# Scratch for rotary queries, laid out by part instead of by head

## The chip, the cores and the metric

The kernel runs on one core of a Trainium2 chip. A core has a matrix engine (PE, TensorE) with a loader for its stationary operand (PEld), a vector engine (DVE), an activation engine (ACT), a general engine (POOL) and a small engine that here only starts transfers (SP). SP, ACT and POOL start DMA transfers; the transfers themselves run on the core's 16 DMA engines. Every engine works through its own list of instructions in order, so an instruction that waits holds up all that stand behind it on the same engine.

The metric is the time of the whole program on the device, in microseconds (us), as the median of several executions.

## The reference

The program is one inference step of a two-layer decoder trunk: 1024 new prompt tokens and 8 sample tokens share the weights. Layer 0 mixes tokens with an mLSTM, layer 1 with multi-head latent attention; each layer ends with a SwiGLU network. The change touches the attention layer alone, and there the queries of the prompt:

```python
c_q, c_kv, k_r = jnp.split(x @ w_in, [Q_LORA, Q_LORA + KV_LORA], axis=-1)
q = (rmsnorm(c_q, g_q) @ w_uq).reshape(B, S, MLA_HEADS, QK_NOPE + QK_ROPE)
q_nope = q[..., :QK_NOPE]                       # 8 heads x 128
q_rope = rope(q[..., QK_NOPE:], pos)            # 8 heads x 64: two halves of 32, turned by the position
s = einsum('bqhc,bkc->bhqk', q_lat, c_kv) + einsum('bqhr,bkr->bhqk', q_rope, k_r)   # q_lat is q_nope @ w_uk
```

Behind it come a causal softmax in blocks of 128 queries, the product with the values, and the output projection. All is float32. The kernel gets the precision on PE by splitting a number into a high part that PE takes as it is and the low rest, so that most products are three matmuls (high x high, low x high, high x low).

## The kernel before, in words

Activations lie transposed, features on the 128 partitions and tokens along the row. The prompt's tokens are worked in three chunks of 344 columns, of which the last holds 336 prompt tokens and the 8 sample tokens.

**The stage of the queries** (`queries`, from L1307) runs through the table `ORDER = "R0 P1 P2 P3 R4 P5 P6 P7 A0"`. `P` makes the plain part of one head (`plain`): three chunks of 9 matmuls. `R0` and `R4` make the rotary part of four heads at once, 4 heads x 32 rows on the partitions, once for each half `e` (`rotary`), besides the plain part of their own head. Each chunk's result goes through `keep` (L1322): ACT writes the high part and DVE the low part of a buffer `qx`, of which there are 12, and then `put_n` (L1331) or `put_r` (L1336) stores it to scratch in DRAM: plain parts to `qn_d`, rotary parts to `qr_d`. A buffer is free for the next chunk when its store has landed. The stores of an entry are issued with the next entry. SP issues the plain stores of heads 0 to 3 and the rotary stores of `R4`; POOL issues the rotary stores of `R0` and the plain stores of heads 4 to 7. Each rotary chunk takes two stores for each half, `i` = 0 for the high and 1 for the low part.

`qr_d` is `[8, P, S]` before: head, then 128 rows, then position. The rows of a head are four parts of 32: high first half, high second half, low first half, low second half (row `64 * i + 32 * e + r`). A store therefore writes 4 heads x 32 rows.

**The attention** (`attention`, from L1446) works in 32 blocks, 8 heads x 4 groups `G` of 256 queries. `load_q` (L1465) fetches a block's queries, one transfer for the plain part (`q`, L1470) and one for the rotary part (`qrr`, 128 rows x 256 columns, L1471), each into one of two buffers. For head 0 ACT issues them, for the others SP, and they are asked for one block ahead. In `prompt` (L1519) the scores take `q` at L1544 to L1546 and `qrr` at L1547 and L1549, with a mask at L1551; DVE takes the maximum (L1552), ACT the exponential (L1561) and the scaling (L1566), PE transposes (L1582) and multiplies with the values (L1602). Between the blocks stand the next head's keys and values (`head_ops`: ACT writes `kt`, `vt` and `spl` at L125 and L126, POOL the low parts at L127) and units for the sample tokens (`sample_units`: gathers from the paged cache on POOL, transposes on DVE, matmuls at L1706 and L1731). `sample_query` (L1406) stands between queries and attention: 16 small matmuls from `qnS` (L1419) and 16 copies of ACT to `qbd` (L1426).

The order of the instructions on each engine isn't written out by hand: a scheduler settles it when the program is built, from priorities and its own costs. A change of a transfer's shape or number can therefore move other instructions.

Of the kernel before, what the change touches and what calls it, by code (L numbers as in the profile page):

```python
# [9 lines left out]
F32 = mybir.dt.float32  # L10
# [8 lines left out]
P = 128  # L19
D = 1024  # L20
KT = D // P
S = 1024
# [66 lines left out]
class Kern:  # L89
# [1217 lines left out]
    def queries(self, qs, cq):  # L1307
        nc = self.nc
        V = nc.vector
        cqh, cql, rc, rn, wT = cq  # L1310
        self.qn_d = self.t(self.dp, [8, 2, P, S], "qn_d")
        self.qr_d = self.t(self.dp, [8, P, S], "qr_d")
        wuq = self.mla_w_uq[0]
        self.qnS = self.t(qs, [P, 8, NS], "qnS")
        self.qrS = self.t(qs, [64, 8, NS], "qrS")
# [17 lines left out]
        def put_r(h0, e):  # L1333
            def f(x, w):
                for i in range(2):
                    (nc.sync if h0 else nc.gpsimd).dma_start(self.qr_d[h0:h0 + 4, 64 * i + 32 * e:64 * i + 32 * e + 32, w], x[:, i])  # L1336
            return f


# [50 lines left out]
        for op in ORDER.split():  # L1390
            h = int(op[1:] or 0)
# [54 lines left out]
    def attention(self, ckh, ckl, kk, kl, cqp, cq):  # L1446
        nc = self.nc
# [17 lines left out]
        def load_q(h, G):  # L1465
            g = slice(G * 256, G * 256 + 256)
            q = self.t(pe, [P, 2, 256], "q", F32R, bufs=2)
            x = self.t(pe, [P, 256], "qrr", F32R, bufs=2)
            e = nc.scalar if h == 0 else nc.sync
            e.dma_start(q.bitcast(F32), self.qn_d[h, :, :, g].rearrange("i p s -> p i s"))  # L1470
            e.dma_start(x.bitcast(F32), self.qr_d[h, :, g])  # L1471
            return q, x

        def head_ops(h):
# [44 lines left out]
        def prompt(h, G, kt, vt):  # L1519
            hv = slice((h % 2) * P, (h % 2) * P + P)  # L1520
            nk = 2 * G + 2

            slot = h * 4 + G if h % 2 == 0 or h == 7 else h * 4 + 3 - G
            q, qx = ahead.pop(slot, None) or load_q(h, G)
            n = slot + 1
            if 0 < slot < 31:
                ahead[n] = load_q(n // 4, n % 4 if n // 4 % 2 == 0 or n >= 28 else 3 - n % 4)
# [393 lines left out]
```

## Time and profile before

| what | us |
|---|---|
| executions, fastest / median / slowest of 3 | 2754.57 / 2765.08 / 2766.46 |
| span of the profiled execution (first to last instruction; its whole time isn't listed apart) | 2743.8 |
| PE busy in the span | 2578.0 (94%) |
| DVE / ACT / POOL busy | 1497.8 / 1178.1 / 877.8 |
| stage of the queries, 1335.0 to 1410.7 | 75.7, PE busy 59.65 |
| 32 blocks of attention, 1410.7 to 1888.0 | 477.3, PE busy 418.04 |

The span is shorter than an execution by what lies before the first and behind the last instruction: 10.8 us against the fastest run, 21.3 us against the median. In views that list instructions, a row has start and duration in us, engine, line, operation, output and inputs; square brackets hold how long the engine sat idle before it, and what ended that. An engine's name with a q (SPq, ACTq) is its sequencer, which issues transfers. Windows give each engine's busy time in a stretch, with the clock that PE was granted (1.00 is full), the busy share of the 16 DMA engines and what they moved.

### The profile page before, as it was taken

To read this page: it belongs to the slowest core of one execution; us is meant where nothing else is said; L and a number is where in the kernel's file an instruction comes from. 1 tells how busy PE (TensorE), PEld (TensorE's weight loads), DVE (VectorE), ACT (ScalarE), POOL (GpSimd) and SP (SyncE) were. 2 spreads that over 40 slices of the span, in tenths; PEclk is the share of its full clock that TensorE was granted. 3 is DMA by queue.
4 is the path that set the end of the run, shared out by engine and by line. 5 is a ranking of instruction groups with operands and counts; after the bars stand their busy time and mean duration, and the time that the engine had idled before them with its cause. 6 is when DMAs were issued, how large, how long until landed. Compare 5 with 4: busy or idle time off the path is not lost.

```text
span 2743.8 us, 51995 instructions
## 1 busy us (share of the span) xinstructions
PE 2578.0 (94%) x20719; PEld 2439.0 (89%) x20719; DVE 1497.8 (55%) x3217; ACT 1178.1 (43%) x2651; POOL 877.8 (32%) x846
## 2 busy tenths in 40 slices
PE   8999988989999999999888889898988999999998
PEld 8998877989999999999776767777988999999998
DVE  4345668863343443366548876686574434444455
ACT  4212334444444444453345455555344444444442
POOL 1000002233333333332325544452223333333343
PEclk9999989999999999999889999898999999999999
DMA  5133455426666556543657767664434655555553
GB/s 186 39 77 92 124 145 128 147 60 128 122 122 120 117 115 123 105 158 102 201 177 293 247 242 242 212 220 150 145 92 99 124 116 123 117 115 116 118 139 103
DMA packets 344937, 384.27 MB, mean 140 GB/s; under 512 B 24362, under 2 KB 296111, under 8 KB 336375
## 3 DMA queue, kind: packets, MB, share of 16 engines
q0 software_dynamic: 42496, 183.35, 28.0%
q1 hardware_dynamic: 277990, 181.25, 22.6%
q10 hardware_dynamic: 24208, 16.36, 2.4%
q8 instruction: 162, 2.65, 0.4%
q14 instruction: 81, 0.66, 0.1%
HBM read 255.17 MB, written 125.70 MB: 139 GB/s over the span
## 4 chain that ended last, share of the span: by engine, by line
PE 66%; DVE 12%; DMA 10%; issue 5%; ACT 4%; POOL 3%; SPq 0%; ACTq 0%; POOLq 0%; DVEq 0%
PE sc L133 10%; PE sc L131 10%; PE sc L132 10%; PE mm L131 5%; PE mm L133 5%; PE mm L132 5%; PE ss L131 5%; PE ss L132 5%; PE ss L133 5%; DVE tt L1699 2%; DMA Gb<-G_d 2%; PE ss L1731 2%; DVE wl L115 1%; DMA nat<-in_cache_latent_dram,idx 1%; DMA qr_d<-qx 1%
## 5 line engine op out<-in xcount | busy, mean ns | idle before, releaser
L131 PE MATMUL ss<-ah,dh 128*128 128x344 f32 x864 | 276.8, 320 | 7.1 <-ACT st L1075 6.7
L1075 ACT COPY st<-ss 128x344 f32<-128x344 f32 x432 | 190.2, 442 | 212.9 <-PE ss L133 173.1
L132 PE MATMUL ss<-al,dh 128*128 128x344 f32 x864 | 276.6, 320 | 1.9 <-POOL al L115 1.9
L133 PE MATMUL ss<-ah,dl 128*128 128x344 f32 x864 | 275.9, 319 | 0.0
L114 ACT ACTIVATE wh<-wr 128x512 fp32r<-128x512 f32 (+2 forms) x152 | 126.1, 830 | 228.2 <-PE mm L132 130.0
L1077 POOL DMA_DIRECT2D x_d<-st x144 | 124.5, 864 | 238.6 <-ACT st L1075 229.1
L131 PEld LDWEIGHTS ss<-ah,dh 128*128 128x128 f32 x864 | 162.4, 188 | 8.3 <-ACT st L1075 7.3
L115 POOL TENSOR_TENSOR al<-u,ah 128x512 fp32r<-128x512 f32 (+1 forms) x84 | 118.2, 1408 | 147.3 <-ACT ah L114 147.2
L132 PEld LDWEIGHTS ss<-al,dh 128*128 128x128 f32 x864 | 162.8, 188 | 2.4 <-POOL al L115 2.4
L115 DVE TENSOR_TENSOR wl<-S,wl 128x512 fp32r<-128x512 f32 x89 | 78.4, 881 | 157.1 <-ACT wl L114 129.4
L133 PEld LDWEIGHTS ss<-ah,dl 128*128 128x128 f32 x864 | 162.3, 188 | 0.0
L1699 DVE STREAM_TRANSPOSE tt<-nat 128x1024 f32<-128x1024 f32 x128 | 153.1, 1220 | 14.5 <-DMA nat<-in_cache_latent_dram,idx 9.3
L1041 DVE TENSOR_TENSOR u<-u,sc 128x260 f32<-128x260 f32 (+1 forms) x168 | 70.8, 421 | 115.2 <-PE sc L133 113.9
L115 DVE TENSOR_TENSOR wh<-S,wh 128x512 fp32r<-128x512 f32 x91 | 68.6, 754 | 119.0 <-ACT wh L114 90.2
L115 DVE TENSOR_TENSOR wl<-wr,wh 128x1024 fp32r<-128x1024 f32 (+2 forms) x83 | 100.2, 1208 | 43.1 <-ACT wh L114 35.2
L1007 POOL TENSOR_TENSOR S<-S,wr 128x512 f32<-128x512 f32 x45 | 62.9, 1398 | 175.0 <-DVE wl L115 88.5
L1000 POOL TENSOR_TENSOR S<-wr 128x512 f32<-128x512 f32 x45 | 61.6, 1369 | 166.0 <-DMA wr<-in_ffn_w_gate_up_dram 163.3
L131 PE MATMUL mm<-zh,wh 128*128 128x344 f32 x320 | 104.6, 327 | 7.6 <-DVE ot L459 7.5
L115 DVE TENSOR_TENSOR dl<-dr,dh 128x256 fp32r<-128x256 f32 x144 | 68.3, 474 | 72.7 <-ACT dh L114 72.7
L132 PE MATMUL mm<-zl,wh 128*128 128x344 f32 x320 | 103.6, 324 | 0.0
L133 PE MATMUL mm<-zh,wl 128*128 128x344 f32 x320 | 103.3, 323 | 0.0
L1009 POOL TENSOR_TENSOR S<-S,wr 128x512 f32<-128x512 f32 x45 | 58.1, 1291 | 132.9 <-DVE wh L115 86.5
(920 smaller groups left out, 9279.0 us busy)
## 6 DMA issues: line engine op xcount, KB each, us to landing
x_d<-st POOLq DMA_DIRECT2D x144, 516.0 KB, 5.6
wr<-in_ffn_w_gate_up_dram SPq DMA_DIRECT2D x98, 512.0 KB
dr<-in_ffn_w_down_dram SPq DMA_DIRECT2D x144, 128.0 KB
wr<-in_mlstm_w_in_dram SPq DMA_DIRECT2D x24, 512.0 KB
wr<-in_mlstm_w_out_dram SPq DMA_DIRECT2D x16, 512.0 KB
wr<-in_mla_w_o_dram SPq DMA_DIRECT2D x15, 512.0 KB
q<-qn_d SPq DMA_DIRECT2D x28, 256.0 KB
x_d<-x SPq DMA_DIRECT2D x16, 260.0 KB
```

The lines of the kernel that those rows point to most:

```text
L114: ins = nc.scalar.activation(hi, src, AF.Copy)
L115: self.low = e.tensor_tensor(lo, src, hi.bitcast(F32), op=ALU.subtract)
L131: mm(ps, wh, xh, start=start, stop=False, **kw)
L132: mm(ps, wh, xl, start=False, stop=False, **kw)
L133: self.last = mm(ps, wl, xh, start=False, stop=stop, **kw)
L1000: G(s, a21, a22, op=ALU.add)
L1007: G(s, s, a11, op=ALU.subtract)
L1009: G(s, s, a12, op=ALU.subtract)
L1041: V.tensor_tensor(u[:, 1], u[:, 1], ps, op=ALU.add)
L1075: nc.scalar.copy(st[:, cs], ps)
L1077: nc.gpsimd.dma_start(self.x_d[:, d], st, accum_op=ALU.add)
L1699: V.transpose(out=tt, in_=src.rearrange("p s (c i) -> p c s i", i=32))
```

## The change

The scratch for the rotary queries becomes `[4, 8 * 32, S]`: part first (`2 * i + e`), then head and row. A store now writes 128 rows of one part that follow each other, 32 for each of four heads. A head's 128 rows of a block then lie in four places, so that a load is four transfers of 32 rows each, one for each part. The bytes are the same, and what lands in `qx` and `qrr` too.

```diff
-        self.qr_d = self.t(self.dp, [8, P, S], "qr_d")
+        self.qr_d = self.t(self.dp, [4, 8 * 32, S], "qr_d")
@@ put_r, the stores
                 for i in range(2):
-                    (nc.sync if h0 else nc.gpsimd).dma_start(self.qr_d[h0:h0 + 4, 64 * i + 32 * e:64 * i + 32 * e + 32, w], x[:, i])
+                    (nc.sync if h0 else nc.gpsimd).dma_start(self.qr_d[2 * i + e, 32 * h0:32 * h0 + P, w], x[:, i])
@@ load_q, the loads
             e.dma_start(q.bitcast(F32), self.qn_d[h, :, :, g].rearrange("i p s -> p i s"))
-            e.dma_start(x.bitcast(F32), self.qr_d[h, :, g])
+            for a in range(4):
+                e.dma_start(x[32 * a:32 * a + 32].bitcast(F32), self.qr_d[a, 32 * h:32 * h + 32, g])
```

From L1471 on, line numbers of the changed kernel are higher by one (the load of `qrr` is L1472, the scores are L1545 to L1552). The scheduler moves instructions as well, from the stage of the queries into the blocks of head 1; behind that the order is as before. Three places:

SP, end of the queries and start of the attention; first the kernel before. `qr_d` is the scratch, `uw_d` holds the weights for keys and values, and the numbers count buffers.

```order
L1336 DMA qr_d_14414<-qx_14884 4x32x336
L1336 DMA qr_d_14414<-qx_14898 4x32x336
L1458 DMA swh_15906<-uw_d_13869 128x2x128
L1458 DMA swl_15908<-uw_d_13869 128x2x128
L1470 DMA q_15591<-qn_d_14413 128x2x256
L1471 DMA qrr_15592<-qr_d_14414 128x256
L1470 DMA q_15911<-qn_d_14413 128x2x256
```

And the changed kernel at the same place:

```order
L1336 DMA qr_d_14414<-qx_14884 128x336
L1336 DMA qr_d_14414<-qx_14898 128x336
L1458 DMA swh_15921<-uw_d_13869 128x2x128
L1458 DMA swl_15923<-uw_d_13869 128x2x128
L1470 DMA q_15603<-qn_d_14413 128x2x256
L1472 DMA qrr_15604<-qr_d_14414 32x256 x4
L1470 DMA q_15926<-qn_d_14413 128x2x256
```

The order on SP is the same; a store has one dimension less, and a load of `qrr` is four issues.

ACT in the stage of the queries, before: `q` and `qrr` are the loads of the first two blocks, `qx` the buffers whose high part ACT writes from the rotary result (`rfa`) or from a PSUM bank (`sc`, `mm`), `wh` a head's weight.

```order
L1470 DMA q_15077<-qn_d_14413 128x2x256
L114 ACTIVATE wh_14598<-wq_14417 128x384
L114 ACTIVATE wh_14657<-wq_14417 128x384
L114 ACTIVATE qx_14561<-rfa_14556 128x336
L1471 DMA qrr_15078<-qr_d_14414 128x256
L114 ACTIVATE qx_14575<-rfa_14570 128x336
L114 ACTIVATE qx_14594<-mm_14584 128x336
L1470 DMA q_15235<-qn_d_14413 128x2x256
L1471 DMA qrr_15236<-qr_d_14414 128x256
L114 ACTIVATE qx_14612<-sc_14602 128x344
L114 ACTIVATE qx_14625<-sc_14615 128x344
L114 ACTIVATE wh_14704<-wq_14417 128x384
```

And with the change:

```order
L1470 DMA q_15077<-qn_d_14413 128x2x256
L114 ACTIVATE wh_14598<-wq_14417 128x384
L114 ACTIVATE wh_14657<-wq_14417 128x384
L114 ACTIVATE qx_14561<-rfa_14556 128x336
L1472 DMA qrr_15078<-qr_d_14414 32x256 x4
L114 ACTIVATE qx_14575<-rfa_14570 128x336
L114 ACTIVATE qx_14594<-mm_14584 128x336
L1470 DMA q_15238<-qn_d_14413 128x2x256
L114 ACTIVATE qx_14612<-sc_14602 128x344
L1472 DMA qrr_15239<-qr_d_14414 32x256 x2
L114 ACTIVATE qx_14625<-sc_14615 128x344
L1472 DMA qrr_15239<-qr_d_14414 32x256
```

Two issues have become eight, and those of the second block now stand among the writes of `qx`.

ACT at the third block of head 0, where it issues the load of `qrr` behind the copies to `qbd`; before:

```order
L1426 COPY qbd_15134<-ql_15155 32x8x2x8 x2
L1471 DMA qrr_15240<-qr_d_14414 128x256
L125 ACTIVATE kt_15209<-mm_15210 128x512
L126 COPY spl_15217<-mm_15210 128x512
L125 ACTIVATE kt_15209<-mm_15221 128x512
L126 COPY spl_15228<-mm_15221 128x512
```

And with the change:

```order
L1426 COPY qbd_15137<-ql_15158 32x8x2x8 x2
L1472 DMA qrr_15246<-qr_d_14414 32x256
L125 ACTIVATE kt_15212<-mm_15213 128x512
L126 COPY spl_15220<-mm_15213 128x512
L125 ACTIVATE kt_15212<-mm_15224 128x512
L126 COPY spl_15231<-mm_15224 128x512
L1472 DMA qrr_15246<-qr_d_14414 32x256 x3
```

Three of the block's four transfers have moved behind four evictions of the next head's keys.

## The prediction

> **What bounds the kernel now.** I read the page first, then the windows around the stores, then PE's and ACT's lists there. The page's chain of waits, by engine and by line:
>
> ```profile
> PE 66%; DVE 12%; DMA 10%; issue 5%; ACT 4%; POOL 3%; SPq 0%; ACTq 0%; POOLq 0%; DVEq 0%
> PE sc L133 10%; PE sc L131 10%; PE sc L132 10%; PE mm L131 5%; PE mm L133 5%; PE mm L132 5%; PE ss L131 5%; PE ss L132 5%; PE ss L133 5%; DVE tt L1699 2%; DMA Gb<-G_d 2%; PE ss L1731 2%; DVE wl L115 1%; DMA nat<-in_cache_latent_dram,idx 1%; DMA qr_d<-qx 1%
> ```
>
> PE bounds the kernel, but `qr_d<-qx`, a store that nothing should wait for, has 1% of the span on the chain. So the question is one stage. Its windows:
>
> ```profile
> core 0: us, PE busy (x) PEld busy (x) DVE busy (x) ACT busy (x) POOL busy (x), PEclk, DMA share, GB/s
> 1335.00:1350.00 15.00, 14.21 (x98) 13.55 (x96) 12.08 (x27) 4.58 (x10) 8.36 (x14) 1.00 0.65 210
> 1350.00:1358.00 8.00, 3.50 (x11) 3.21 (x12) 3.74 (x13) 1.54 (x4) 1.60 (x3) 0.58 0.81 176
> 1358.00:1368.00 10.00, 7.43 (x46) 6.99 (x45) 3.04 (x11) 2.31 (x7) 1.33 (x2) 1.00 0.77 202
> 1368.00:1377.00 9.00, 8.90 (x47) 8.78 (x47) 6.08 (x17) 3.48 (x9) 0.00 (x0) 0.81 0.97 341
> 1377.00:1396.00 19.00, 18.84 (x120) 18.56 (x119) 18.09 (x54) 7.65 (x18) 4.79 (x7) 1.00 0.52 142
> 1396.00:1410.70 14.70, 6.77 (x51) 6.68 (x50) 2.28 (x8) 2.08 (x5) 2.71 (x5) 0.84 0.56 183
> 1410.70:1423.00 12.30, 12.23 (x60) 10.13 (x61) 3.89 (x16) 4.85 (x13) 2.67 (x4) 0.50 0.56 195
> ```
>
> PE has two holes, 1350 to 1368 and 1396 to 1410.7, and near each its granted clock is low (0.58, 0.81, 0.50). PE's list names three gaps:
>
> ```profile
> 1354.49 0.65 PE L131 MATMUL sc<-cqh,wh 128*128 128x344 f32 x1 [5.29 <-ACT wh L114]
> ...
> 1367.55 0.42 PE L131 MATMUL sc<-cqh,wh 128*128 128x344 f32 x1 [2.57 <-ACT wh L114]
> ...
> 1410.77 1.45 PE L1419 MATMUL ss<-qnS,wT 128*128 128x8 f32 x6 [8.00 <-DVE qnS L1382]
> ```
>
> Together 15.86 us. What ACT did meanwhile:
>
> ```profile
> 1348.52 0.44 ACT L114 ACTIVATE qx<-sc 128x344 fp32r<-128x344 f32 x1
> 1353.37 0.37 ACTq L1470 DMA_DIRECT2D q<-qn_d  x1
> 1353.92 0.94 ACT L114 ACTIVATE wh<-wq 128x384 fp32r<-128x384 f32 x2 [4.96 <-DMA qr_d<-qx]
> 1355.02 2.70 ACTq L1471 DMA_DIRECT2D qrr<-qr_d  x1
> 1362.52 0.37 ACTq L1470 DMA_DIRECT2D q<-qn_d  x1
> 1363.08 3.15 ACTq L1471 DMA_DIRECT2D qrr<-qr_d  x1
> 1366.28 0.81 ACT L114 ACTIVATE qx<-sc 128x344 fp32r<-128x344 f32 x2 [7.69 <-issue]
> ...
> 1409.22 0.46 ACT L114 ACTIVATE qx<-sc 128x344 fp32r<-128x344 f32 x1 [7.44 <-DMA qr_d<-qx]
> ```
>
> The first two gaps stand behind ACT's loads of `q`, which wait until stores to `qn_d` have landed, and behind issues of 2.70 and 3.15 us. The third is a `qx` buffer that a store to `qr_d` still holds. The views of `qr_d` and `qn_d` give the issues (min/median/max ns), and one more window what the engines move:
>
> ```profile
> L1471 SPq DMA_DIRECT2D qrr<-qr_d x28: 332/408/1186, 1434.8 to 1864.9; - x28
> L1336 POOL DMA_DIRECT2D qr_d<-qx x12: 667/674/736, 1343.5 to 1359.8; - x12
> L1336 SPq DMA_DIRECT2D qr_d<-qx x12: 508/1843/5281, 1378.7 to 1405.7; - x12
> L1471 ACTq DMA_DIRECT2D qrr<-qr_d x4: 327/1548/3152, 1355.0 to 1434.5; - x4
> ```
>
> ```profile
> L1331 SPq DMA_DIRECT2D qn_d<-qx x12: 359/380/1090, 1345.9 to 1375.4; - x12
> ```
>
> ```profile
> 1380.00:1383.00 3.00, 3.00 (x21) 3.00 (x20) 2.76 (x7) 0.49 (x2) 0.77 (x1) 1.00 0.27 72
> ```
>
> From 1380 to 1383 little but SP's stores to `qr_d` is under way, and a share of 0.27 is 4 of 16 engines. From 1368 to 1377, with stores to `qn_d` (128 rows outermost), it is 0.97 and 341 GB/s. I conclude that a store whose outermost dimension is 4 heads runs on 4 engines. SP's issues then stall (median 1843 ns, to 5281), and the chain stays on these stores for 23.85 us:
>
> ```profile
> 1349.75 12.75 DMA qn_d<-qx
> ...
> 1385.27 23.85 DMA qr_d<-qx x2
> 1409.22 0.47 ACT qx L114
> ```
>
> **The change part by part.** A store of 128 equal rows should use all 16 engines as those to `qn_d` do.
>
> *Gap 1 (5.29).* ACT waits for a store issued about 1345.9 and landed at 1353.35, some 7.5 us. Stores that share the engines with less land sooner:
>
> ```profile
> x_d<-st POOLq DMA_DIRECT2D x144, 516.0 KB, 5.6
> ...
> uw_d<-wh POOLq DMA_DIRECT2D x4, 512.0 KB, 3.2
> uw_d<-wl POOLq DMA_DIRECT2D x4, 512.0 KB, 4.7
> ```
>
> Those are larger and take 3.2 to 5.6. I take 4.5 for the 344 KB here, so 3.0 less. Bounds 0 to -4.3.
>
> *Gap 2 (2.57).* The store that lands after 12.75 us lands, at 4.5, by 1354.3, before ACT comes to its load. The two issues of 5.85 us in all become eight; at the calm 0.41 of the median above they are 3.3. The gap goes: -2.57, bound 0.
>
> *Gap 3 (8.00).* At 341 GB/s a store of 172 KB takes 0.5 us on 16 engines, so twelve of them leave no queue, and SP's issues fall to about 0.5. Behind the last chunk PE has other matmuls while ACT and DVE evict it: -8.0, bound -5.0.
>
> *The clock.* PE's busy time times the missing clock: 3.50 x 0.42 = 1.5, 8.90 x 0.19 = 1.7, 12.23 x 0.50 = 6.1. The second comes back; of the first half (a 2.3 us gap stays); of the third 3.5, since ACT and DVE limit parts of that window. Sum -6.0, bounds 0 and -9.3.
>
> *The third block's load.* ACT issues it late, and PE waits:
>
> ```profile
> 1428.03 0.40 ACTq L1471 DMA_DIRECT2D qrr<-qr_d  x1
> ...
> 1430.40 0.61 ACT L126 COPY spl<-mm 128x512 f32<-128x512 f32 x1
> ```
>
> ```profile
> 1430.22 0.50 PE L1547 MATMUL sc<-kk,qrr 128*128 128x512 f32 x1 [0.93 <-DMA qrr<-qr_d]
> ```
>
> From issue to use it is 1430.22 - 1428.43 = 1.8 us. By the new order three of four issues stand behind the eviction that ends at 1431.01, so the last ends at 1431.01 + 3 x 0.40 = 1432.2 and PE starts at 1434.0, 3.8 later. Two matmuls moved ahead of it fill 0.9. ACT also loses 3 x 0.40 here and as much at the fourth block. I take +3.5, bounds 0 and +5.
>
> *The other 28 loads.* SP has three issues more in each, 28 x 3 x 0.41 = 34 us, which is the price if they lay bare. What covers them is that a load is asked for a block ahead. The tightest I found by pairing issues with first uses:
>
> ```profile
> 1763.93 0.42 SPq L1471 DMA_DIRECT2D qrr<-qr_d  x1
> ```
>
> ```profile
> 1768.95 0.41 PE L1547 MATMUL sc<-kk,qrr 128*128 128x128 f32 x1
> ```
>
> It ends at 1764.35 and has 4.6 us; it needs 1.8 + 1.2. Behind SP's loads stand those of the next `q` and weights, later by 1.2 and asked for just as early. +0.5, bounds 0 and +3.
>
> *The moved instructions.* From the queries into head 1 several engines' orders change. No row prices that: 0, with 5 either way as an estimate from the gaps of 0.6 to 2.6 us that PE has there.
>
> Sum: -3.0 - 2.57 - 8.0 - 6.0 + 3.5 + 0.5 = -15.6. The span goes from 2743.8 to 2728.2; with the 21.3 us between the span and the median run, **2749.5**. (Beside the fastest run, 10.8 above the span, it would be 2739.) All bounds on one side give -29, on the other +8.
>
> **The rivals.**
>
> *Only the third gap closes* (17%). In the first half POOL issues the rotary stores; its transfers may already be spread well, four engines for one store and the next four for the next. For it: 1350 to 1358 has a DMA share of 0.81, not 0.27. Against it: at that share only 176 GB/s move, where 0.97 moves 341. Then gaps 1 and 2 and their clock stay: -8.0 - 3.5 + 3.5 + 0.5 = -7.5, 2757.6. The Trainium skill has this as a rule ("DMA: Bandwidth & Descriptors", section "Why a DMA increments its semaphore by 16 and not by 1"): the number of engines is the largest up to 16 that divides both sides' slowest dimension, the lowest-numbered for SP and ACT, and for GpSimd consecutive ones from a cursor that goes round. The window at 1380 agrees for SP; no row here shows which engines POOL's stores used.
>
> *Four loads cost as four* (9%). If a block's transfers landed one after the other, 1.8 us each, a load would need 5.4 more. The third block then loses 5.4 more, blocks with 4 to 5 us of room up to 3 each: +8 on top, -7.6, 2757.5. Against it: the sixteen-engine stores overlap freely from 1368 to 1377. The Trainium skill speaks for it ("DMA: Bandwidth & Descriptors", section "Rules for kernel authors"): coalesce small transfers, since under 64 KB one pays mostly overhead; these are 32 KB. It also gives about 2.0 us as a fixed cost, by which the sum would come out about the same as with the 1.8.
>
> *The change doesn't do what it says* (7%): the stores stay slow for another reason, the bytes or the 4 KB steps between rows. Then only costs remain, +4: 2769. Against it: `qn_d` has the same steps at 341 GB/s.
>
> *Slower: ACT's eight loads in the stage of the queries* (9%). If the long issues (2.70, 3.15) come from the plain stores' backlog and hold for a transfer of any size, eight take 25.2 us instead of 5.85, ACT stands between PE and its weights, and gaps 1 and 2 grow by 19.4. With +3.0 for the clock behind them, +4.0 from the loads of the attention and -11.5 from gap 3 and its clock: +14.9, 2780. It decides from the price at which -11.5 + 4 + 3 + (8p - 5.85) is 0, p = 1.3 us for a load. Against it: stores to `qn_d` at the same time took 380 ns at the median.
>
> **How the numbers follow.** Forecast 58%, rivals 17, 9, 7 and 9. A measurement of this kernel can tell about 0.5%, 13.8 us, from no change. The forecast lies 1.8 beyond that with some 8 us of spread (the moved instructions, the clock, runs that differ by 12), so 0.6 of its 58% is faster: 0.35, and with a fifth of the first two rivals 0.40. Slower holds two thirds of its own rival and the tails of the others, 0.10. The same has the rest, 0.50. The range goes from the forecast with 5 us of luck in the moved instructions and runs that lie at the span as the fastest does, 2743.8 - 15.6 - 5 + 10.8 = 2734, up to the third rival, 2768.
>
> **What would show it.** SP's issues of `qr_d<-qx` near 0.5 us, ACT's of `qrr` near 0.4; the chain without 23.85 us of stores; no PE gap above 3 us before 1400; the small matmuls of L1419 about 16 us earlier, at a clock near 1; a wait for `qrr` of 3 to 4 us in the third block. Wrong would be: a DMA share near 0.25 while only rotary stores run; ACT still held at the load of `q` for 4 us; PE waiting for `qrr` in many blocks; or the 16 us gained by 1411 and lost again before 1530, where the moved instructions end.

## The result

The changed kernel takes 2751.41 us (median of 18 executions, 2743.77 to 2762.20), the kernel before 2764.24 us beside it (18, 2754.57 to 2771.17): a ratio of 0.9960, 95% interval 0.9948 to 0.9972, and 12.8 us less by the medians. The ratio is not the quotient of the two medians (0.9960 is 11.1 us); the two ways of counting differ by up to 3 us in the runs below. Two later series gave 0.9944 (0.9923 to 0.9965) and 0.9935 (0.9917 to 0.9954). The forecast was 15.6 us less, 2749.5 us. The first series lies inside the 0.5% that was taken as the bound, the later two a little beyond it.

The profiled execution of the changed kernel has a span of 2760.4 us, 16.6 *more* than that of the kernel before, and its own time is 2762.20, the slowest of the 18. The time of an execution is its span and 1.7 to 3.3 us more, in all series and kernels. So the first profile of the kernel before, with a span of 2743.8, belongs to an execution of about 2746 us, quicker than all 18 that were timed: the 10.8 and 21.3 us named before the prediction are mostly not time around the span, but the distance of this quick execution from the timed ones. The two profiles can't be compared as wholes, only place by place.

Windows of the first profiles, from the first write of `qx` to the last matmul of L1419 and from there on to the fourth store of `ot_d` (the attention's result, one store for a block); first the kernel before:

```profile
1342.67:1414.78 72.11, 55.99 (x330) 54.48 (x329) 41.12 (x117) 20.90 (x48) 18.28 (x26) 0.87 0.71 210
1414.78:1482.97 68.19, 55.62 (x600) 44.16 (x600) 45.21 (x88) 39.73 (x95) 31.72 (x31) 0.89 0.67 243
```

The changed kernel, with the window of the first half, and the attention cut once more at the third store:

```profile
core 0: us, PE busy (x) PEld busy (x) DVE busy (x) ACT busy (x) POOL busy (x), PEclk, DMA share, GB/s
1350.00:1358.00 8.00, 4.81 (x30) 4.53 (x29) 6.14 (x16) 2.62 (x7) 3.23 (x6) 0.91 0.98 342
1347.73:1404.23 56.50, 52.88 (x330) 52.15 (x329) 41.76 (x117) 21.56 (x48) 16.60 (x26) 0.94 0.77 272
1404.23:1455.32 51.09, 37.35 (x311) 27.83 (x310) 24.88 (x53) 26.51 (x63) 22.24 (x22) 0.83 0.62 217
1455.32:1483.27 27.95, 22.20 (x290) 17.21 (x290) 18.94 (x40) 13.29 (x36) 12.47 (x12) 0.93 0.71 257
```

The queries went from 72.11 to 56.50 us: 15.6 less, PE's idle time from 16.1 to 3.6 and its busy time from 56.0 to 52.9, at a clock of 0.94 in place of 0.87. In the window from 1350 to 1358 the DMA engines move 342 GB/s, where the kernel before had 176. The stretch behind them went from 68.19 to 51.09 + 27.95 = 79.04, 10.9 more. The issues of the stores (min/median/max ns) are what the prediction asked for, SP's 352 ns instead of 1843:

```profile
L1472 ACTq DMA_DIRECT2D qrr<-qr_d x16: 308/377/648, 1357.0 to 1426.2; - x16
L1336 POOL DMA_DIRECT2D qr_d<-qx x12: 540/542/553, 1348.5 to 1361.6; - x12
L1336 SPq DMA_DIRECT2D qr_d<-qx x12: 319/352/488, 1378.0 to 1388.5; - x12
```

Of the three gaps the first is left, at 3.19 instead of 5.29. Two others stand behind the queries now:

```profile
1357.48 0.65 PE L131 MATMUL sc<-cqh,wh 128*128 128x344 f32 x1 [3.19 <-ACT wh L114]
...
1421.09 0.58 PE L1545 MATMUL sc<-kt,q 128*128 128x512 f32 x1 [2.58 <-ACT wr L1562]
...
1432.60 0.77 PE L1548 MATMUL sc<-kk,qrr 128*128 128x512 f32 x1 [3.15 <-DMA qrr<-qr_d]
```

The first profiles alone thus leave two theories. Theory A: the stores' spread is the gain, and what seems lost behind the queries is mostly a difference between executions. Theory B: the four loads and the moved instructions cost 10 us and more behind the queries, and the gain is the remainder.

### The profile page after: what moved, and what is told of

Its sections match the earlier page's. It is cut to its first block, busy times and chain, and to the rows that moved or that the text cites. A ratio compares the mean times of both kernels' runs of the same rounds, so it can differ in the third digit from the quotient of the medians.

```text
span 2760.4 us, 52158 instructions
## 1 busy us (share of the span) xinstructions
PE 2588.2 (94%) x20719; PEld 2438.5 (88%) x20719; DVE 1495.5 (54%) x3217; ACT 1178.5 (43%) x2651; POOL 876.8 (32%) x846
## 4 chain that ended last, share of the span: by engine, by line
PE 69%; DVE 13%; DMA 8%; ACT 4%; issue 4%; POOL 2%; another core or an unknown queue 0%; SPq 0%; ACTq 0%; POOLq 0%; DVEq 0%
PE sc L133 10%; PE sc L131 10%; PE sc L132 9%; PE mm L131 5%; PE mm L133 5%; PE mm L132 5%; PE ss L131 5%; PE ss L132 5%; PE ss L133 5%; DMA Gb<-G_d 2%; DVE tt L1700 2%; PE ss L1732 2%; PE ss L1707 2%; DVE wl L115 2%; PE mm L1603 1%
## 5 line engine op out<-in xcount | busy, mean ns | idle before, releaser
L115 DVE TENSOR_TENSOR wh<-S,wh 128x512 fp32r<-128x512 f32 x91 | 68.2, 749 | 118.7 <-ACT wh L114 90.8
L1007 POOL TENSOR_TENSOR S<-S,wr 128x512 f32<-128x512 f32 x45 | 62.9, 1398 | 174.4 <-DVE wl L115 88.1
L1707 PE MATMUL ss<-tt,qbd 128*32 128x128 f32 x2560 | 95.4, 285 | 16.2 <-DVE tt L1700 10.9
```

Of the source, the lines that this page charges most:

```text
L115: self.low = e.tensor_tensor(lo, src, hi.bitcast(F32), op=ALU.subtract)
L1007: G(s, s, a11, op=ALU.subtract)
L1707: nc.tensor.matmul(psS[32 * j:32 * j + 32, u * P:u * P + P], self.qbd[:, b, cb], tt[:, c, 4 * j:4 * j + 4].rearrange("p s k -> p (s k)"), ...
```

## The experiments

Three series of four kernels, each series on one chip beside the kernel before; the medians of the kernel before were 2761.07, 2760.37 and 2742.67 us. "Queries" and "to 4th store" are the two stretches above, in each kernel's profiled execution.

| series | kernel | ratio to before (95%) | median, us against before | queries | to 4th store |
|---|---|---|---|---|---|
| first | before | | | 72.1 | 68.2 |
| first | changed | 0.9960 (0.9948-0.9972) | -12.8 | 56.5 | 79.0 |
| 1 | before again | 1.0003 (0.9989-1.0017) | +1.1 | 66.8 | 76.4 |
| 1 | loads only | 1.0008 (0.9995-1.0021) | +3.5 | 70.8 | 75.4 |
| 1 | stores only, one load | 1.0005 (0.9988-1.0023) | +4.1 | 56.4 | 79.8 |
| 1 | stores by head | 0.9941 (0.9920-0.9961) | -15.9 | 54.7 | 76.1 |
| 2 | changed again | 0.9944 (0.9923-0.9965) | -14.1 | 56.0 | 77.0 |
| 2 | first half of the stores by head | 0.9982 (0.9970-0.9995) | -4.9 | 64.8 | 75.5 |
| 2 | by head, ACT's loads in four | 0.9938 (0.9915-0.9960) | -19.5 | 54.8 | 77.1 |
| 2 | by head, SP's loads in four | 0.9954 (0.9936-0.9972) | -11.0 | 55.0 | 76.2 |
| 3 | second half of the stores by head | 0.9945 (0.9926-0.9965) | -13.6 | 60.3 | 64.4 |
| 3 | before, third time | 0.9996 (0.9978-1.0014) | -0.6 | 70.0 | 68.1 |
| 3 | stores by head again | 0.9936 (0.9918-0.9955) | -15.2 | 55.9 | 63.8 |
| 3 | changed, third time | 0.9935 (0.9917-0.9954) | -16.6 | 56.0 | 71.1 |

### The kernel before, again

No edit.

> The kernel before, once more, for a second profile of it and for what two series of one kernel differ by. In the two profiles at hand the changed kernel is 15.6 us faster through the queries (first qx to last small matmul of L1419: 72.11 us before, 56.50 after) and then loses 13.7 us in block 3 and about 17 us from block 10 to 28, although its median run is 12.8 us faster. Theory A (spread): the later losses belong to the one execution that was profiled (2760.4 us of span, against a median run of 2751.4); then this profile has the 72 us again within 2 us, but its later blocks lie up to 15 us from those of the first profile. Theory B (loads): they belong to the change; then this profile of the kernel before agrees with its first one within 3 us at block 3 and within 5 us at block 28. Time: 0.999 to 1.001 of the kernel before.

Its windows, queries, to the fourth store, and from there to the fourteenth:

```profile
1338.64:1405.40 66.76, 54.77 (x330) 53.81 (x329) 41.08 (x117) 20.86 (x48) 18.27 (x26) 0.88 0.75 222
1405.40:1481.78 76.38, 59.74 (x597) 46.21 (x598) 44.02 (x88) 39.92 (x95) 31.72 (x31) 0.88 0.65 238
1481.78:1661.22 179.44, 152.87 (x1962) 120.58 (x1961) 133.55 (x286) 92.05 (x244) 89.77 (x88) 0.97 0.67 234
```

The same kernel takes 76.38 us to the fourth store where its first profile took 68.19, and 179.44 to the fourteenth where that took 169.87. Set at the first `qx`, it is at the 28th store 23.7 us behind its own first profile, more than the changed kernel (15.6). So losses of this size come without the change: theory A. Its numbers for the queries missed: 66.8 isn't within 2 us of 72.1.

### The loads alone

```diff
-            e.dma_start(x.bitcast(F32), self.qr_d[h, :, g])
+            for a in range(4):
+                e.dma_start(x[32 * a:32 * a + 32].bitcast(F32), self.qr_d[h, 32 * a:32 * a + 32, g])
```

> The load part alone: the scratch and the stores of the kernel before, a block's load as four transfers of 32 rows. PE, ACT and DVE have then the very order of the changed kernel. Theory A: the stores are still slow (SP's issues near 1.8 us, 72 us through the queries or a little more because ACT issues eight loads there) and the loads cost little behind: +3 to +6 us, ratio 1.001 to 1.002. Theory B: the loads and the moved instructions cost 13.7 us in block 3 and go on costing: +14 to +30 us, ratio 1.005 to 1.011. A third one (the moved instructions, not the stores, brought the 12.8 us): -8 to -13 us, ratio 0.995 to 0.997.

1.0008, +2.2 us by the ratio, with -1.4 to +5.8 left by its interval: theory A, and the moved instructions did not bring the gain. But with the stores still slow, ACT's issues among them stall. SP's stores, and ACT's loads of the first two blocks:

```profile
L1336 SPq DMA_DIRECT2D qr_d<-qx x12: 547/1977/5169, 1376.0 to 1402.1; - x12
```

```profile
1351.47 4.07 ACTq L1472 DMA_DIRECT2D qrr<-qr_d  x1
1355.63 4.22 ACTq L1472 DMA_DIRECT2D qrr<-qr_d  x3
...
1363.60 2.64 ACTq L1472 DMA_DIRECT2D qrr<-qr_d  x1
```

The eight take 11.9 us together, where the two of the kernel before took 5.8 and the eight of the changed kernel 2.9.

### The stores alone

```diff
-            for a in range(4):
-                e.dma_start(x[32 * a:32 * a + 32].bitcast(F32), self.qr_d[a, 32 * h:32 * h + 32, g])
+            e.dma_start(x.bitcast(F32), self.qr_d[:, 32 * h:32 * h + 32, g])
```

(against the changed kernel: its scratch and stores, but one load.)

> The store part alone: the changed scratch and stores, a block's load as one transfer whose outermost dimension is the 4 parts. PE and DVE have the very order of the kernel before. Theory A: the queries take 56 to 58 us instead of 72, and nothing else moves unless a load on four engines is late: a load of 128 KB at the 72 GB/s of 1380 to 1383 takes 1.8 us of moving instead of under 1, and SP's issue may stall as the stores' did. -14 to -16 us, ratio 0.994 to 0.995, and up to +5 us on that if the loads are late. Theory B: -20 to -30 us, ratio 0.989 to 0.993, since the losses behind the queries go too. The third (moved instructions): within 2 us of the kernel before.

1.0005: nothing gained, although the queries took 56.42 us. The single load has the four parts outermost, and is late. Its issues, and PE's waits at the third and fourth block:

```profile
L1471 SPq DMA_DIRECT2D qrr<-qr_d x28: 512/542/841, 1414.6 to 1874.5; - x28
```

```profile
1409.41 0.50 PE L1547 MATMUL sc<-kk,qrr 128*128 128x512 f32 x1 [2.41 <-DMA qrr<-qr_d]
...
1423.70 0.80 PE L1547 MATMUL sc<-kk,qrr 128*128 128x512 f32 x1 [4.71 <-DMA qrr<-qr_d]
```

An issue is 542 ns instead of 408, and PE waits 10.4 us for `qrr` in four places, where the kernel before's first profile has 1.3 in two. The late load was named in the expectation, at +5; here the whole gain of some 15 us is missing. Of that only the 10.4 us are seen, in an execution (2749.20 us) that was the quickest of its twelve; where the slower ones lost more stays open. So the cut of the load into four is needed: without it the change is worth nothing that can be measured.

### The stores by head

```diff
                 for i in range(2):
-                    (nc.sync if h0 else nc.gpsimd).dma_start(self.qr_d[h0:h0 + 4, 64 * i + 32 * e:64 * i + 32 * e + 32, w], x[:, i])
+                    for k in range(4):
+                        (nc.sync if h0 else nc.gpsimd).dma_start(self.qr_d[h0 + k, 64 * i + 32 * e:64 * i + 32 * e + 32, w], x[32 * k:32 * k + 32, i])
```

(against the kernel before; its scratch and single loads stay.)

> The scratch and the single load of the kernel before, but each rotary store issued as four, one for each head, of 32 rows. PE's order is that of the kernel before. If a store of 32 rows spreads over the 16 engines as one of 128 does, the queries get as short as in the changed kernel, and no load costs anything. Against it stand three issues more for each of 24 stores: 36 on POOL by 0.67 us is 24 us of POOL's sequencer, whose later work is then up to 20 us later, and 36 on SP by 0.35 us. Theory A: -12 to -16 us, ratio 0.994 to 0.996; a rival (POOL's sequencer becomes the wait of the queries): -8 to 0, ratio 0.997 to 1.000, with the first two gaps still there.

0.9941, the queries in 54.73 us: theory A. PE has the order of the kernel before here, so the gain is the stores' alone. The 36 issues more on POOL raise its busy time in the queries from 18.3 to 33.7 us. PE doesn't wait for that: its one gap above 0.6 us in the queries is 2.02.

### The changed kernel, again

No edit.

> The changed kernel once more, for a second profile and beside the other kernels of this series. Its first profile lay 9 us above its median run. Theory A (what was lost behind the queries in that profile is a spread between executions, most of it of the granted clock, and only some 3 to 5 us are the loads'): ratio 0.995 to 0.997 again, and a profile whose way from the first qx to the last use of qrr is up to 15 us shorter than the first one's, with the waits of PE for qrr again at 4 to 7 us in all. Theory B (the loss in the third and fourth block is the change's own): the way from the last small matmul of L1419 to the store of block 3 is again 51 us, against 37 us in the kernel before's first profile.

0.9944. Its way from the first `qx` to the last use of `qrr` is 556.8 us, 2.4 less than in its first profile and not up to 15: theory A's number missed. The changed kernel's first profile was an ordinary one there (the kernel before in series 1 took 567.3); the one that differs is the first profile of the kernel before, at 544.8. PE's waits for `qrr`, 6.5 us in all, lie within the 4 to 7 of theory A. The way from L1419 to the third store is 49.3 us, in agreement with theory B's number. But the kernel before needs 44.8 there, not 37, once it runs as in series 1: the change costs 4.5 us at that place, not 14, and at the fourth store 0.6 of it is left (77.0 against 76.4).

### The stores of the first half alone

```diff
+                    if not h0:
+                        for k in range(4):
...
+                    else:
...
```

(one store for each head where `h0` is 0, the store of the kernel before otherwise.)

> As the stores by head, but only POOL's rotary stores of heads 0 to 3 (R0) go out in fours; SP's of heads 4 to 7 (R4) stay as before, and so do the loads. If both halves pay as the prediction had it, this half gives the first two gaps and the clock behind them, -3.0 - 2.6 - 2.5 = -8 us, ratio 0.997. If POOL's plain stores were spread over the 16 engines already, four for one store and the next four for the next, it gives 0 to +3 us (36 issues more on POOL), ratio 1.000 to 1.001, and the two gaps stay. If nearly all of the 15.9 us come from this half, -13 us or more, ratio 0.995.

-4.9 us, between the -8 and the 0 that were expected. PE's gaps:

```profile
1349.51 0.46 PE L131 MATMUL sc<-cqh,wh 128*128 128x344 f32 x1 [1.97 <-ACT wh L114]
...
1401.78 0.38 PE L1423 MATMUL ss<-qnS,wT 128*128 128x8 f32 x1 [8.79 <-DVE qnS L1386]
```

The first gap is 1.97, the second is gone, the third stays. So POOL's stores did hold up the queries, though they weigh less than SP's.

### The loads of ACT, and those of SP, in four

Both are the stores by head, with these lines

```diff
-            e.dma_start(x.bitcast(F32), self.qr_d[h, :, g])
+            for a in (range(4) if h == 0 else range(1)):
+                o = slice(32 * a, 32 * a + 32) if h == 0 else slice(0, P)
+                e.dma_start(x[o].bitcast(F32), self.qr_d[h, o, g])
```

for ACT's loads, and with `if h` in place of both `if h == 0` for SP's.

> The stores by head (which gave -15.9 us) and the loads of head 0, which ACT issues, as four transfers each; SP's 28 loads stay single. PE, DVE and ACT then have the changed kernel's order but for a handful of rows, so that this is ACT's sixteen loads together with the moved instructions. Theory A: this is the whole of the 3 to 5 us by which the changed kernel is behind the stores by head: -11 to -13 us, ratio 0.995 to 0.996, PE waiting 4 to 7 us for qrr in the third and fourth block. Theory B (block 3's 13.7 us are the change's own): -2 us, ratio 0.999. Rival (the loads on SP are what costs): -15 to -17 us, ratio 0.994.

> The stores by head, ACT's four loads single, and SP's 28 loads as four transfers each. The orders are those of the stores by head but for SP's issues and four rows of PE. Theory A: 84 issues more, 34 us of SP's sequencer, cost what the prediction put in for them, +0.5, at most +3: -13 to -16 us, ratio 0.994 to 0.995, PE's waits for qrr in blocks 5 to 31 as without them. Rival (four loads cost as four): +3 to +8 on the stores by head, -8 to -13 us, ratio 0.995 to 0.997, with waits for qrr in several blocks.

0.9938 and 0.9954 beside 0.9941 without either (from series 1): neither part of the loads has a cost that these intervals show. ACT's part, at -19.5 us, is better than all three expectations, and PE waits 1.8 us for `qrr` in it, not 4 to 7. SP's part, at -11.0 us, falls into the rival's range by its time, but not by the waits that the rival needs: PE waits 2.6 us for `qrr` in two places, as it does in the stores by head without it. The place of the cost is seen, though: ACT's loads in four bring the changed kernel's order, and with it 49.2 us to the third store, where the stores by head took 44.6 and SP's loads in four 44.2. At the fourth store 77.1 stand against 76.1 and 76.2. With only 1.8 us of waiting for `qrr`, the moved instructions are left as the reason for most of those 4.6 us.

### The stores of the second half alone

```diff
+                    if h0:
+                        for k in range(4):
...
+                    else:
...
```

> The other half alone: only SP's rotary stores of heads 4 to 7 (R4) go out in fours, POOL's of R0 stay as before; all engines but SP keep the order of the kernel before. The first half alone gave -4.9 us, both together -15.9. If the halves add up, -11 us, ratio 0.996: the gap before the small matmuls of L1419 (7 to 8 us) and the half clock around it go, the two gaps behind ACT's loads stay, and the way from the first qx to the last matmul of L1419 is 61 us (66.8 to 72.1 with the slow stores, 64.8 with the first half, 54.7 with both). If instead a gap closed early only moves the wait on to the next, the second half alone gives all, -14 to -16, ratio 0.9945.

0.9945 and -13.6 us, between the -11 of halves that add up and the -14 to -16 of one that gives all; the interval (-9.6 to -20) holds both. Its first gap, and the queries:

```profile
1358.41 0.65 PE L131 MATMUL sc<-cqh,wh 128*128 128x344 f32 x1 [6.26 <-ACT wh L114]
```

```profile
1345.63:1405.93 60.30, 53.75 (x330) 52.32 (x329) 41.19 (x117) 20.94 (x48) 18.26 (x26) 0.94 0.81 245
```

The queries took 60.3 us, as halves that add up would have it, and the first gap stayed, at 6.26; a second one of 0.6 us or more is not in this profile, though it was expected. The 4.4 us by which both halves are quicker there (55.9 in the same series) are not told apart in the time: -13.6 against -15.2. The twelve stores of SP are most of what this change gains.

### The kernel before for the third time, the stores by head and the changed kernel beside it

> The kernel before for a third profile. Its first two differ by 5.4 us through the queries (72.1, 66.8) and by 8.2 us from there to the store of block 4 (68.2, 76.4), while all other kernels took 75.4 to 79.8 for the second. If the first profile was the odd one, this one shows 66 to 71 and 75 to 77 us; if both ways are common to this kernel, 68 to 70 for the second stretch shows up here again. Time: 0.999 to 1.001.

> The stores by head again, beside the changed kernel on the same chip: is it faster than the changed kernel, as -15.9 against -12.8 and -14.1 us would have it? If the loads in four cost the 3 to 5 us of theory A: 0.994 here and 0.9955 there. If they cost nothing that can be told: ratios within 0.001 of each other.

> The changed kernel beside the stores by head, and for a third profile: 0.9945 to 0.996; first qx to last matmul of L1419 56 to 57 us at a clock of 0.94 to 0.95; from there to the store of block 3 49 to 51 us, to that of block 4 77 to 79 us.

All three ran on one chip. The profiled execution of the kernel before (2750.38 us) is the slowest of its twelve, 8 us above their median; that of the changed kernel (2726.01) lies at its median. Windows of queries, to the third store, to the fourth, to the fourteenth; the kernel before:

```profile
1343.95:1413.93 69.98, 54.68 (x330) 53.16 (x329) 41.02 (x117) 20.83 (x48) 18.26 (x26) 0.89 0.72 215
1413.93:1450.83 36.90, 30.17 (x231) 23.39 (x232) 17.46 (x44) 25.36 (x62) 17.48 (x18) 0.89 0.60 219
1450.83:1482.03 31.20, 26.28 (x370) 21.36 (x369) 26.60 (x44) 14.36 (x34) 14.22 (x14) 0.84 0.72 267
1482.03:1654.89 172.86, 151.50 (x1960) 122.64 (x1958) 133.22 (x286) 91.92 (x244) 89.85 (x88) 0.95 0.71 251
```

and the changed kernel:

```profile
1339.85:1395.89 56.04, 52.65 (x330) 51.92 (x329) 41.38 (x117) 21.54 (x48) 16.58 (x26) 0.95 0.79 277
1395.89:1441.17 45.28, 36.47 (x310) 27.44 (x310) 22.52 (x51) 26.39 (x63) 19.17 (x19) 0.84 0.59 211
1441.17:1467.02 25.85, 22.93 (x295) 18.86 (x294) 20.90 (x42) 13.23 (x36) 13.89 (x15) 0.93 0.77 270
1467.02:1632.57 165.55, 147.43 (x1953) 114.89 (x1954) 127.59 (x282) 92.01 (x242) 88.30 (x87) 0.97 0.74 258
```

The queries give 13.9 us, the way to the third store takes 8.4 back, the next block returns 5.4 of these; 3.0 stay. From there to the fourteenth store the changed kernel is 7.3 us quicker, so that from L1419 to there it has lost nothing: 236.7 us against 241.0, and 254.6 (series 2) against 255.8 (series 1). Beside the stores by head it is 3.5 us behind here (233.2) and 3.2 ahead in the earlier series (257.8), so a lasting cost of the loads isn't seen. On this chip 68 us to the fourth store are common (68.1, 64.4, 63.8 without ACT's loads in four), and the first profile of the kernel before was of this kind, while the changed kernel's first profile (79.0 and 177.7) looks like those of series 1 and 2. Which chip either came from isn't listed, so that reading is argued; that the kernel before alone differs by 8 us here between the series is measured.

The stores by head are no faster than the changed kernel: 0.9936 and 0.9935, as expected if the loads cost nothing that can be told. For the kernel before, 70.0 and 68.1 us say that both ways are common. The changed kernel's queries came as expected (56.0 us at a clock of 0.95), but not its ratio, below the 0.9945 to 0.996, nor the ways to the third and fourth store, 45.3 and 71.1 instead of 49 to 51 and 77 to 79: those numbers were taken from the earlier profiles. No kernel that was run beats it by more than the intervals.

## Why the prediction was right, point by point

The forecast held: -15.6 forecast, -12.8, -14.1 and -16.6 measured. What it had named as its refutation, 16 us gained by 1411 and lost again before 1530, is what the first two profiles show (15.6 gained, 10.9 of it lost by the fourth store); but these two profiles come from unlike executions, of about 2746 and of 2762 us. Beside the later profiles of the kernel before 0.6 us (series 2 against series 1) and 3.0 us (both in series 3) are lost there. That the sum came so near is in part luck. In the queries it had -16.0 (gaps -13.6, clock -2.5), where the last series shows -13.9; at their end and behind them it had +0.5, made of 3.5 from the clock that did not come, and of 4.0 for the loads that no later profile shows as a lasting cost. By its steps, with the two profiles of the last series:

*The stores use more engines.* Right for SP's. The view of DMA queues gives packets, MB and share of the 16 engines; q1 is the queue of SP's transfers. The kernel before from 1380 to 1383 (first profile), and the changed one from 1370 to 1372, each while almost nothing but the rotary stores moves:

```profile
q1 hardware_dynamic: 154, 0.21, 25.6%
```

```profile
q1 hardware_dynamic: 473, 0.56, 80.4%
```

These are 4.1 and 12.9 engines. POOL's stores land sooner too. Median from issue to landing of POOL's stores (the view of DMA issues, last column in us), kernel before and then the changed one:

```profile
qr_d<-qx POOLq DMA_DIRECT2D x8, 172.0 KB, 8.8
...
qr_d<-qx POOLq DMA_DIRECT2D x4, 168.0 KB, 9.6
```

```profile
qr_d<-qx POOLq DMA_DIRECT2D x8, 172.0 KB, 4.8
...
qr_d<-qx POOLq DMA_DIRECT2D x4, 168.0 KB, 2.3
```

That POOL's stores had too few engines is not shown. Its queue is q0; while it stores rotary parts, beside loads of weights, the kernel before (first profile, 1344 to 1353) and the changed one (1341 to 1349) have:

```profile
q0 software_dynamic: 954, 1.47, 55.3%
```

```profile
q0 software_dynamic: 563, 1.95, 64.8%
```

With the stores as they were, this queue kept 8.8 engines busy, but an MB took 54 us of engine time (0.553 x 16 x 9 / 1.47), with the change 43. So in this half the engines did not lie idle, they were slower, with more packets for fewer bytes; why stays open.

The stores by head, with the old addresses, gain as much as the new layout, and the load with the four parts outermost loses it. So it is the outermost dimension of a transfer, not the rows' place in the scratch, as the third rival would have had it.

*The gaps.* The kernel before, in the last series, and the one that the changed kernel keeps:

```profile
1356.32 0.65 PE L131 MATMUL sc<-cqh,wh 128*128 128x344 f32 x1 [5.82 <-ACT wh L114]
...
1367.92 0.42 PE L131 MATMUL sc<-cqh,wh 128*128 128x344 f32 x1 [0.91 <-ACT wh L114]
...
1409.91 0.38 PE L1419 MATMUL ss<-qnS,wT 128*128 128x8 f32 x1 [8.32 <-DVE qnS L1382]
```

```profile
1349.60 0.66 PE L131 MATMUL sc<-cqh,wh 128*128 128x344 f32 x1 [3.23 <-ACT wh L114]
```

Gap 1: -3.0 forecast, -2.6 here and -2.1 in the first profiles. The prediction took ACT's wait there for one on SP's store to `qn_d`; its own row for ACT (4.96 us) names a store to `qr_d`, which POOL issues, and the halves bear that out: 1.97 with POOL's rotary stores cut, 6.26 with SP's. Gap 3: -8.0 forecast, -8.3 here, and gone. Gap 2 was taken too large: -2.57 from a profile in which it happened to be that; it is 0.91 here, and in the profile of series 1 no gap of 0.6 us or more stands there.

*The clock.* -6.0 forecast, mis-placed. In the queries PE's busy time falls by 2.0 us (54.68 to 52.65) and by 3.1 in the first profiles, where 2.5 had been put in. The 3.5 from the window behind 1410.7 did not come. The prediction took the half clock there for a consequence of the third gap. With the gap gone it is still there. Here are, before and with the change, the 12.3 us that end 8.3 us behind the last matmul of L1419:

```profile
1409.90:1422.20 12.30, 12.29 (x62) 10.21 (x62) 3.83 (x15) 4.84 (x13) 2.61 (x4) 0.52 0.56 191
```

```profile
1391.90:1404.20 12.30, 12.30 (x71) 10.17 (x70) 3.13 (x12) 5.14 (x13) 1.50 (x3) 0.58 0.47 154
```

The clock is 0.52 with the gap ahead of it and 0.58 without, and PE is busy all the time in both. The mean granted clock of the executions of series 2 and 3 was 0.9732 before and 0.9754 and 0.9755 with the change; (1 - clock) times the span falls by 6.5 and 6.7 us. That is not time saved: some 5 of it lie in the queries ((1 - 0.89) x 69.98 against (1 - 0.95) x 56.04), in part in the third gap, in which PE has nothing to do.

*The third block's load.* +3.5 forecast, 0 to +5. At the third store it is 8.4 here, and 4.5 in series 2; at the fourth 3.0 and 0.6, and at the fourteenth nothing. The late load is one part of it, 2.44 us of PE behind the last of four issues:

```profile
1418.07 0.31 ACTq L1472 DMA_DIRECT2D qrr<-qr_d  x1
```

```profile
1423.82 0.47 PE L1548 MATMUL sc<-kk,qrr 128*128 128x512 f32 x1 [2.44 <-DMA qrr<-qr_d]
```

*The moved instructions.* 0 forecast, 5 either way. They are the larger part of this stop, as ACT's loads in four show above with 1.8 us of waiting. In DVE's new order five transposes of the sample tokens' cache stand ahead of the sum and reciprocal (`sm`) of the running block, and the first of them waits for a gather; ACT stands idle for `sm`:

```profile
1423.91 1.25 DVE L1700 STREAM_TRANSPOSE tt<-nrp 128x1024 f32<-128x1024 f32 x1 [4.08 <-DMA nrp<-in_cache_k_rope_dram,idx]
1425.08 4.58 DVE L1700 STREAM_TRANSPOSE tt<-nat 128x1024 f32<-128x1024 f32 x4
1429.59 0.19 DVE L1564 TENSOR_TENSOR sm<-sm 128x1 f32<-128x1 f32 x2
```

```profile
1430.48 0.83 ACT L1567 ACTIVATE wr<-wr,sm 128x640 f32<-128x640 f32 x1 [8.82 <-DVE sm L1565]
```

The transposes are then done, and the next block has them ahead of time, and 5.4 us come back there. That nothing is left of it at the end fits the 0; that a stall of nearly 9 us and its return lie within them was not seen.

*The other 28 loads.* +0.5 forecast, at most 3. The stores by head with SP's loads in four and those without differ by 0.9954 against 0.9941, 3.6 us, within their intervals. PE's waits for `qrr` are the same 2.6 us in both profiles, which speaks for the forecast; by the times alone a cost of up to some 11 us isn't excluded.

*The 21.3 us "between the span and the median run".* Wrong as a reason. Around the span lie 1.7 to 3.3 us; the rest was the distance of one quick execution, perhaps of another chip, to the median. The number came out because adding it put the gain on the median; the bound at the fast end, which took 10.8 as what lies around, was not sound.

*The rivals.* That only the third gap closes is half right: the second half of the stores alone gives nearly the whole time, but -13.6, not -7.5, and the first half is worth -4.9 by itself with its gap at 1.97. The rule of the Trainium skill on which that rival stood ("DMA: Bandwidth & Descriptors", section "Why a DMA increments its semaphore by 16 and not by 1"), that a transfer gets the largest number of engines up to 16 that divides both sides' slowest dimension, agrees with SP's 25.6 and 80.4% above and with the late load of the third experiment. What it says of GpSimd's turn of engines does not contradict the 55.3% of POOL's queue; but the first gap did shrink when POOL's stores were cut, so that this rival's consequence failed even if its condition held. Four loads did not cost as four: the +8 put in for that is not there, and the Trainium skill's advice to coalesce small transfers ("DMA: Bandwidth & Descriptors", section "Rules for kernel authors") is not borne out here: the one large load with 4 parts outermost was the dear one, and 112 loads in place of 28, with 32 and 128 rows outermost, cost nothing that can be told. And ACT's eight loads are no trouble once the stores are quick, 2.9 us in all; with slow stores they took 11.9, half of the 25.2 that the rival had put in.

## What to carry to other kernels

Look at a transfer's outermost dimension on its way out and on its way in: here 4 heads outermost stalled SP's issues for up to 5.3 us, and with the same shape on the load nothing of the gain was left. Cutting the stores into one for each head, without a new layout, did as well (0.9936 against 0.9935), and most of that is SP's twelve stores (0.9945). Before a profile is used for a sum, set its own time against the timed executions, and take a second one: a gap of one profile (2.57 us here) may be 0.9 or nothing in the next.

## What was not expected of the hardware

The granted clock goes with the gaps of the queries. They ran at 0.87 to 0.89 in all profiles with the slow stores of the second half (72.1, 66.8, 70.8, 64.8, 70.0 us) and at 0.94 to 0.96 in all others, and PE's busy time for the same 330 matmuls is 53.9 to 56.0 us in the former and 52.3 to 53.8 in the latter. So the gaps went with some 2 us more in the matmuls beside them (54.9 against 52.8 on average); that the gap causes the low clock is argued from this, and no run changed the clock alone. Nor does every low clock need a gap: that at the start of the attention stays, at 0.58, with none ahead of it. What brings it there is open.

The series differ in place, not only in whole. The kernel before was 2761.07 us on one chip and 2742.67 on another. Of the 13.6 us between its two profiled spans there (2762.0 and 2748.4), 6.6 lie between the fourth and the fourteenth store (179.4 and 172.9 us), where the DMA engines moved 234 GB/s on the one and 251 on the other. Each chip was used in one series, so that the chip as the reason is argued.
